# The last 256 features of a feed-forward input product, as a narrow seven-product group

## The chip, the cores and the metric

One Trainium2 chip, one of its cores. The metric is the device time of one execution in microseconds (us). The kernel before took 850.61 us (median of 3 runs, 849.67 to 852.32).

## The reference, cut to what matters

One decoder layer on 512 tokens of width 1024: a mixer block of three branches, merged and put through `w_out`, and then a feed-forward part (FFN) with 2816 hidden features.

```python
x = x + merged @ w_out[l]                      # (512, 1024)
h2 = rmsnorm(x, norm_ffn_g[l])
ffn_g, ffn_u = jnp.split(h2 @ w_ffn_in[l], 2, axis=-1)      # 1024 -> 2 x 2816
x = x + (jax.nn.silu(ffn_g) * ffn_u) @ w_ffn_out[l]         # 2816 -> 1024
return rmsnorm(x, final_norm_g)
```

All of it is float32. A product of two float32 matrices is computed in three terms of a shorter type (float32r): each operand is split into a rounded part `hi` and a remainder `lo`, and hi x hi, hi x lo and lo x hi are added up.

## The kernel before, in words

The kernel is a list of operations with their dependences. A planner in the kernel file (`schedule`, L253) gives every operation an engine, a start by its own table of costs, and a buffer, and the program then runs each engine's list in that fixed order. Priorities set by `at(...)` decide between operations that could start at the same time.

Weights come in units of 512 KB (128 partitions x 1024 numbers). A unit is loaded by a DMA on SP's queue into a buffer called `raw` (two of them) or `ch` (six), cast to `hi` by ScalarE (ACT in the profile) and subtracted to `lo` by VectorE (DVE) (`unit_loads`, L529). There are three buffers for `hi` and three for `lo`, so the cast of a unit waits until TensorE (PE) is done with the unit three before it.

The FFN's input product runs as a seven-product scheme (Strassen's, in Winograd's form): the tokens are cut in two halves of 256, the 1024 inputs in two halves, and a group of 512 gate features and the 512 up features that belong to them are the two halves of the output. Seven products of halves take the place of eight (`PRODUCTS`, L98, in the order p1, p3, p5, p2, p6, p7, p4). Their input operands are the normalized tokens (`xh`, `xl`) and sums of them (`c1`, `c2`), made on VectorE and split once. Their weight operands are sums of blocks of `w_ffn_in`. These sums are made by the DMA: a plain load of one block into a `ch` buffer, and later accumulating DMAs on POOL's queue (GpSimd) that add further blocks (`accum`, L456). In an ordinary group two such running sums serve all products: x for p1, p5, p6, p4 and y for p3, p7; p2 is a plain load (`_group`, L68). Each is two units wide, so a group has 14 units, and a unit 12 matmuls of 128 x 512: two token tiles, two blocks of 128 inputs, three terms (`seven`, L1159). An accumulation into a running sum has to wait until the split of the sum's last state is done.

Products are collected in PSUM: p1 with p6 and p3 with p7 in tiles called `g`, p5 with p4 and p2 in tiles called `m`. `evict` (L1206) reads them out, applies the row norms `rstd2`, Silu and the gate product, and 16 transposes per group bring the result to features on partitions (`feat`, tiles `a`), with copies by ScalarE.

Five groups make 2560 features. The last 256 features (`LEFT`, features 20 and 21 of 128) run before the groups as plain products over all 512 tokens (L1133): gate and up for each, four products of 24 matmuls of 128 x 512, with the row norms broadcast to `RB2` (L1125 to L1128) and the result written straight to `feat`.

The output product follows in two sections of the same scheme (`SECTIONS`, L90), the first over features 0 to 11 of 128, the second over 12 to 21. Its operands are made from the tiles `a` in buffers `R` (36 of them). 32 of the 36 hold the input product's operands, so most become free only as the last group of the input product is done with them.

Of the kernel before, what the change touches and what calls it, by code (L numbers as in the profile page):

```python
# [13 lines left out]
ALU = mybir.AluOpType  # L14
AX = mybir.AxisListType

P = 128
# [3 lines left out]
KD = 8  # L21
DFF = 2816
# [14 lines left out]
UNITS = []  # L37


def _units():  # L40
# [12 lines left out]
    for d in W_OUT:  # L53
        UNITS.append(("col", "w_out", d * P))
    for f in LEFT:
        UNITS.append(("col", "w_ffn_in", f * P))
        UNITS.append(("col", "w_ffn_in", DFF + f * P))
    for n in range(len(UNITS)):
        STREAM.append(("raw", n, 2))

    for g in range(5):
        _group(g, "w_ffn_in", [[(4 * h + 2 * j, 4 * h + 2 * j + 1) for j in range(2)] for h in range(2)],
               (g * 512, DFF + g * 512))
    for s, halves in enumerate(SECTIONS):
        _group(5 + s, "w_ffn_out", halves, (0, 512))
# [18 lines left out]

LEFT = (20, 21)
W_OUT = (0, 4, 1, 5, 2, 6, 3, 7)
# [11 lines left out]
STREAM = []  # L100
# [374 lines left out]
def tile_block(ctx: ExitStack, tc: tile.TileContext, xT_d, w_d, wif_d, pp_d, nb_d, fg_d, cf_d, cm_d, out_d):  # L475
# [53 lines left out]
    def unit_loads():  # L529
        chains, before = {}, []  # L530
        for u, (kind, w, width, *more) in enumerate(STREAM):
            parts = []
            for n, sl in enumerate([slice(0, 512), slice(512, 1024)] if u < 2 else [slice(0, 512 * width)]):
# [3 lines left out]
                with at(URGENT, -1, u + 0.2 * n):  # L537
                    if kind == "add":
                        raw = chains[more[0]]
                        E.accum(raw, w_d[w, :, sl])  # L540
                    else:
                        raw = new("F" if u < 2 else "ch" if kind == "new" else "raw", f"raw{u}_{n}", shape)
                        E.load(raw, w_d[w, :, sl])
# [548 lines left out]
    rstd2 = const("rstd2", [P, NC])  # L1092
    acc2, RB2 = tmp("sqacc2"), keep("RB2")
    for n, d in enumerate(W_OUT):
# [29 lines left out]
    with at(URGENT, 0):  # L1124
        rms_cols(acc2, rstd2, "ffn")  # L1125
        rb2 = psm("rb2")
        bcast_cols(rb2, rstd2)
        E.copy(RB2, rb2)  # L1128


    av = [new("a", f"a{i}", (P, 2, S)) for i in range(KF // 2)]
    feat = [av[f // 2][:, f % 2, :] for f in range(KF)]
    for f in LEFT:  # L1133
        g, u = tmp(f"ffsg{f}"), tmp(f"ffsu{f}")
        for nm, t in (("g", g), ("u", u)):
            p = psg(f"ff{nm}{f}")
            hi, lo = unit()
            product(p, hi, lo, xh, xl, KD, alloc=[t])
            with at(URGENT, 0):
                E.tt(t, p, RB2, ALU.mult)  # L1140
        with at(CHAIN):
            E.act(g, g, "Silu")
            E.tt(feat[f], g, u, ALU.mult)

    x2n = [[xr[i * 4 + c] for i in range(2)] for c in range(NC)]
# [12 lines left out]

    def seven(tag, widths, operand, evict, by_token=False):  # L1159

# [3 lines left out]
        for name, op, m in PRODUCTS:  # L1164
            for j, w in enumerate(widths):
                hi, lo = unit()
                ah, al = operand(op, j)
                if by_token and name == PRODUCTS[-1][0]:
                    last.append((j, w, hi, lo, ah, al))
                    continue  # L1170
                with at(GEMM, count[1]):
                    for t in range(2):
                        for kk in range(w):
                            sl = slice(kk * 512, (kk + 1) * 512)
                            first = j == kk == 0
                            fresh = name in ("p1", "p3", "p5", "p2")
                            E.mm(acc[m][t], ah(kk, t), hi[:, sl], first and fresh, False, skip=not fresh)
                            E.mm(acc[m][t], ah(kk, t), lo[:, sl], False, False, skip=not fresh)
                            E.mm(acc[m][t], al(kk, t), hi[:, sl], False,
                                 j == len(widths) - 1 and kk == w - 1, skip=not fresh)  # L1180
            for t in range(2):
                for j, w, hi, lo, ah, al in last:
                    with at(GEMM, count[1]):
                        for kk in range(w):
                            sl = slice(kk * 512, (kk + 1) * 512)
                            for a, b in ((ah, hi), (ah, lo), (al, hi)):
                                end = b is hi and a is al and j == len(widths) - 1 and kk == w - 1
                                E.mm(acc[m][t], a(kk, t), b[:, sl], False, end, skip=True)
                with at(URGENT, 0):
                    evict(name, t, acc[m][t])  # L1190

    for g in range(5):
        def operand(op, j):
# [12 lines left out]
        def evict(name, t, p):  # L1206
            r1, r2 = rstd2[:, t:t + 1], rstd2[:, 2 + t:3 + t]
            if name == "p1":
                held["c11", t] = new("Y", f"c11_{g}_{t}")
                E.copy(held["c11", t], p)  # L1210
            elif name == "p3":
                held["c12", t] = tmp(f"c12_{g}_{t}")
                E.copy(held["c12", t], p)
# [6 lines left out]
            elif name == "p7":  # L1220
                x, u = held["c12", t], tmp(f"c22_{g}_{t}")
                held["c22", t] = u
# [3 lines left out]
            else:  # L1226
                x, u = tmp(f"c21_{g}_{t}"), held["c22", t]
                E.tt(x, p, u, ALU.subtract)
# [3 lines left out]

        seven(f"fi{g}", (2, 2), operand, evict)
        nat = [held[n, t] for n in ("c12", "c22") for t in range(2)]
        with at(CHAIN):
            for q in range(4):
                pt = psm(f"at{g}_{q}")
# [143 lines left out]
def _layout(inp):  # L1381
# [4 lines left out]
    for i, (kind, name, *a) in enumerate(UNITS):  # L1386
# [3 lines left out]
        elif kind == "rows":  # L1390
            pack[i] = 0
            for n, r in enumerate(a[0]):
                pack[i, :, n * 512:(n + 1) * 512] = m[r * P:(r + 1) * P, a[1]:a[1] + 512]
        elif kind == "nat":
# [69 lines left out]
```

## Time and profile before

| | before |
|---|---|
| runs | 849.67, 850.61, 852.32 us |
| the profiled execution's own time | 851.7 us |
| its span, first to last instruction | 849.9 us |
| TensorE busy | 837.8 us (99%) |
| weight loads busy (PEld) | 694.7 us (82%) |
| VectorE busy | 644.4 us (76%) |
| ScalarE busy | 446.6 us (53%) |
| POOL busy | 60.0 us (7%) |
| mean granted clock of TensorE | 0.998 of full speed |
| DMA | 110.72 MB, 130 GB/s on average |

Matmuls are pipelined, and the duration of one includes its way through the array: 128 x 512 has a mean of 393 ns, while they follow each other much faster. So what counts for the time is the distance from one start to the next, which is read from the timeline or the chain of waits by dividing a stretch by its count. In the chain the name before a line number is the tile that is written: "PE g L374" are matmuls of `mm` into tiles `g`, "PE m L380" are transposes. Names of tiles are without their numbers: R are operands in float32r, hi and lo the halves of the weights.

### The profile page before, as it was taken

To read this page: it belongs to the slowest core of one execution; us is meant where nothing else is said; L and a number is where in the kernel's file an instruction comes from. 1 tells how busy PE (TensorE), PEld (TensorE's weight loads), DVE (VectorE), ACT (ScalarE), POOL (GpSimd) and SP (SyncE) were. 2 spreads that over 40 slices of the span, in tenths; PEclk is the share of its full clock that TensorE was granted. 3 is DMA by queue.
4 is the path that set the end of the run, shared out by engine and by line. 5 is a ranking of instruction groups with operands and counts; after the bars stand their busy time and mean duration, and the time that the engine had idled before them with its cause. 6 is when DMAs were issued, how large, how long until landed. Compare 5 with 4: busy or idle time off the path is not lost.

```text
span 849.9 us, 10774 instructions
## 1 busy us (share of the span) xinstructions
PE 837.8 (99%) x3952; PEld 694.7 (82%) x3952; DVE 644.4 (76%) x1139; ACT 446.6 (53%) x702; POOL 60.0 (7%) x76
## 2 busy tenths in 40 slices
PE   8999999999999999999999999999999999999996
PEld 6888888888878888888888888888888888888875
DVE  7868899999999985226228686476757578989977
ACT  6355243334798984331333565446454657655545
POOL 1000000000000000000000000212121212121220
PEclk9999999999999999999999999999999999999999
DMA  9322122222221223322225722779798988797773
GB/s 320 128 73 84 51 75 75 75 76 81 92 98 52 76 74 99 100 93 83 101 96 198 246 100 73 137 190 179 187 180 189 179 184 181 196 207 187 149 131 117
DMA packets 33748, 110.72 MB, mean 130 GB/s; under 512 B 3744, under 2 KB 4128, under 8 KB 33696
## 3 DMA queue, kind: packets, MB, share of 16 engines
q1 hardware_dynamic: 24480, 77.53, 27.1%
q0 software_dynamic: 9216, 32.51, 22.0%
q8 instruction: 31, 0.51, 0.3%
q14 instruction: 21, 0.17, 0.1%
HBM read 107.93 MB, written 2.10 MB: 129 GB/s over the span
## 4 chain that ended last, share of the span: by engine, by line
PE 94%; DVE 4%; DMA 1%; issue 0%; ACT 0%; SPq 0%; ACTq 0%; DVEq 0%
PE g L374 71%; PE m L374 20%; PE m L380 2%; DVE xf L412 1%; DVE lo L405 1%; DMA raw<-in_w_dram 1%; DVE R L405 1%; DMA F<-in_w_dram 1%; DVE F L412 0%; ACT hi L396 0%; DVE R L430 0%; DVE xf L420 0%; SPq L453 0%; DVE T L405 0%; DVE F L405 0%
## 5 line engine op out<-in xcount | busy, mean ns | idle before, releaser
L374 PE MATMUL g<-R,hi 128*128 128x512 f32 x1200 | 298.7, 393 | 0.0
L374 PEld LDWEIGHTS g<-R,hi 128*128 128x128 f32 x1200 | 222.5, 188 | 44.3
L405 DVE TENSOR_TENSOR lo<-raw,hi 128x1024 fp32r<-128x1024 f32 x98 | 119.2, 1216 | 97.1 <-PE g L374 63.2
L374 PE MATMUL g<-hi,R 128*128 128x512 f32 x608 | 187.3, 393 | 0.9 <-DVE lbt L434 0.9
L396 ACT CAST hi<-raw 128x1024 fp32r<-128x1024 f32 x98 | 102.6, 1047 | 160.0 <-PE g L374 120.3
L374 PE MATMUL g<-R,lo 128*128 128x512 f32 x600 | 157.9, 395 | 0.0
L405 DVE TENSOR_TENSOR lo<-ch,hi 128x1024 fp32r<-128x1024 f32 (+1 forms) x96 | 113.7, 1188 | 53.7 <-ACT hi L396 46.4
L396 ACT CAST hi<-ch 128x1024 fp32r<-128x1024 f32 (+1 forms) x96 | 98.2, 1024 | 89.6 <-PE g L374 39.0
L374 PEld LDWEIGHTS g<-hi,R 128*128 128x128 f32 x608 | 114.3, 189 | 24.4 <-ACT T L389 1.1
L374 PEld LDWEIGHTS g<-R,lo 128*128 128x128 f32 x600 | 111.1, 188 | 21.8
L374 PE MATMUL m<-hi,R 128*128 128x512 f32 x372 | 118.4, 391 | 0.1
L374 PE MATMUL g<-lo,R 128*128 128x512 f32 x304 | 114.7, 397 | 0.0
L459 POOL DMA_DIRECT2D ch<-in_w_dram x64 | 55.6, 878 | 687.4 <-DVE lo L405 687.4
L374 PEld LDWEIGHTS m<-hi,R 128*128 128x128 f32 x372 | 69.9, 188 | 14.7 <-ACT hi L396 0.5
L374 PE MATMUL m<-lo,R 128*128 128x512 f32 x186 | 73.0, 392 | 0.2 <-DVE lo L405 0.2
L374 PEld LDWEIGHTS g<-lo,R 128*128 128x128 f32 x304 | 57.7, 190 | 11.9 <-DVE lo L405 0.3
L412 DVE SCALAR_TENSOR_TENSOR xf<-xf,pp,xf 128x511 f32<-128x511 f32 (+29 forms) x60 | 42.6, 725 | 0.1
L396 ACT CAST R<-T 128x512 fp32r<-128x512 f32 (+1 forms) x48 | 28.3, 601 | 27.4 <-DVE T L405 11.5
L374 PEld LDWEIGHTS m<-lo,R 128*128 128x128 f32 x186 | 34.9, 188 | 7.4 <-DVE lo L405 0.5
L389 ACT ACT_TABLE_LOAD x31 | 39.8, 1283 | 1.2 <-PEq L1453 0.7
L405 DVE TENSOR_TENSOR R<-T,R 128x512 fp32r<-128x512 f32 (+1 forms) x48 | 30.8, 662 | 0.7 <-ACT R L396 0.7
L389 ACT ACTIVATE xf<-g,pp 128x512 f32<-128x512 f32 x27 | 18.6, 690 | 15.6 <-PE g L374 15.5
(207 smaller groups left out, 800.6 us busy)
## 6 DMA issues: line engine op xcount, KB each, us to landing
raw<-in_w_dram SPq DMA_DIRECT2D x97, 512.0 KB, 3.3
ch<-in_w_dram POOLq DMA_DIRECT2D x60, 512.0 KB, 5.5
ch<-in_w_dram SPq DMA_DIRECT2D x30, 512.0 KB, 4.5
F<-in_xT_dram SPq DMA_DIRECT2D x12, 256.0 KB, 4.9
out_dram<-F SPq DMA_DIRECT2D x8, 256.0 KB, 2.1
F<-in_w_dram SPq DMA_DIRECT2D x4, 256.0 KB, 5.5
xf<-in_xT_dram SPq DMA_DIRECT2D x4, 256.0 KB, 7.0
xf<-in_cm_dram SPq DMA_DIRECT2D x4, 256.0 KB, 5.2
```

What stands on the lines that cost most here:

```text
L374: return self.pr.add("PE", cost, [lhsT, rhs, *after], [out], lambda: self.nc.tensor.matmul(r(out), lhsT=r(lhsT), rhs=r(rhs), start=start, ...
L380: lambda: self.nc.tensor.transpose(r(out), r(in_), r(ident)))
L389: lambda: self.nc.scalar.activation(r(out), r(in_), getattr(AF, func), bias=r(bias), scale=r(scale), **{k: r(x) for k, x in kw.items()}),
L396: lambda: self.nc.scalar.copy(out=r(out), in_=r(in_)))
L405: return self.pr.add("V", (66 + free_size(out)) / 0.96, [a, b, *after], [out], lambda: self.nc.vector.tensor_tensor(out=r(out), in0=r(a), ...
L412: lambda: self.nc.vector.scalar_tensor_tensor(r(out), r(a), r(s), r(b), op0=op0, op1=op1))
L459: return self.pr.add("G", 1000.0, [out], [out], lambda: self.nc.gpsimd.dma_start(out=r(out), in_=src, accum_op=ALU.add), lat=_prod(out.sha ...
```

## The change

The features 20 and 21 are no longer computed by plain products ahead of the groups. They become a sixth group at the end of the input product, of 256 gate and 256 up features, with the same seven products. Its unit holds four blocks of 128 inputs x 256 features, so a product has one unit and 24 matmuls of 128 x 256. Each product's weight sum is made by itself: a load of the first block and accumulating DMAs for the others, one for p5 and p7, two for p6, three for p4, none for p1, p3 and p2. The broadcast of the row norms goes, and the evictions and 8 transposes of the new group come, with half-width tiles. The planner makes a new order of everything from the end of the `w_out` product on.

```diff
-    for f in LEFT:
-        UNITS.append(("col", "w_ffn_in", f * P))
-        UNITS.append(("col", "w_ffn_in", DFF + f * P))
...
+    _last_group((5 * 512, DFF + 5 * 512))
...
+def _last_group(cols):
+    b = [[], []]
+    for h in range(2):
+        for n in range(2):
+            b[h].append(len(UNITS))
+            UNITS.append(("rows", "w_ffn_in", range(4 * h, 4 * h + 4), cols[n], 256))
+    (b11, b12), (b21, b22) = b
+    blocks = dict(p1=[b11], p3=[b22], p5=[b11, b12], p2=[b21], p6=[b11, b12, b22], p7=[b12, b22],
+                  p4=[b11, b12, b22, b21])
+    for prod, _, _ in PRODUCTS:
+        STREAM.append(("sum", blocks[prod], 2))
...
+                    elif kind == "sum":
+                        raw = new("ch" if len(w) > 1 else "raw", f"raw{u}_{n}", shape)
+                        E.load(raw, w_d[w[0], :, sl])
+                        for more in w[1:]:
+                            E.accum(raw, w_d[more, :, sl])
...
-        rb2 = psm("rb2")
-        bcast_cols(rb2, rstd2)
-        E.copy(RB2, rb2)
...
-    for f in LEFT:
-        g, u = tmp(f"ffsg{f}"), tmp(f"ffsu{f}")
-        for nm, t in (("g", g), ("u", u)):
-            p = psg(f"ff{nm}{f}")
-            hi, lo = unit()
-            product(p, hi, lo, xh, xl, KD, alloc=[t])
-            with at(URGENT, 0):
-                E.tt(t, p, RB2, ALU.mult)
-        with at(CHAIN):
-            E.act(g, g, "Silu")
-            E.tt(feat[f], g, u, ALU.mult)
...
-    def seven(tag, widths, operand, evict, by_token=False):
+    def seven(tag, widths, operand, evict, by_token=False, cols=512):
...
+                w = w * 512 // cols
...
-                            E.mm(acc[m][t], ah(kk, t), hi[:, sl], first and fresh, False, skip=not fresh)
+                            E.mm(acc[m][t][:, :cols], ah(kk, t), hi[:, sl], first and fresh, False, skip=not fresh)
...
-    for g in range(5):
+    for g in range(6):
+        cols = 512 if g < 5 else 256
...
-        seven(f"fi{g}", (2, 2), operand, evict)
+        seven(f"fi{g}", (2, 2) if g < 5 else (2,), operand, evict, cols=cols)
...
-            for q in range(4):
+            for q in range(cols // P):
```

How the order moves, at three places. On TensorE, the end of the `w_out` product (its last matmul is the row that reads lo_1_81) and what follows; before, first the left-over feature 20, whose weights hi stand behind the tokens R:

```order
L374 MATMUL g_2_85<-R_25_132,lo_1_81 128x512
L374 MATMUL g_3_86<-R_30_137,hi_2_79 128x512
L380 MATMUL m_1_88<-cf_59,F_7_150 128x128
L380 MATMUL m_1_88<-cf_59,F_3_146 128x128
L380 MATMUL m_1_88<-cf_59,F_9_152 128x128
L380 MATMUL m_3_90<-cf_59,F_7_150 128x128
L380 MATMUL m_3_90<-cf_59,F_3_146 128x128
L380 MATMUL m_3_90<-cf_59,F_9_152 128x128
L374 MATMUL g_3_86<-R_32_139,hi_2_79 128x512
```

The same place now:

```order
L385 MATMUL g_2_85<-R_25_132,lo_1_81 128x512
L385 MATMUL g_3_86<-hi_2_79,R_30_137 128x512
L391 MATMUL m_1_88<-cf_59,F_7_150 128x128
L391 MATMUL m_1_88<-cf_59,F_3_146 128x128
L391 MATMUL m_1_88<-cf_59,F_9_152 128x128
L391 MATMUL m_3_90<-cf_59,F_7_150 128x128
L391 MATMUL m_3_90<-cf_59,F_3_146 128x128
L391 MATMUL m_3_90<-cf_59,F_9_152 128x128
L385 MATMUL g_3_86<-lo_2_82,R_30_137 128x512
```

The matmuls between the transposes of the residual are now those of p1 of the first group (hi and lo are the moving operand, the token tile R the weights of the array).

On POOL's queue, the accumulating DMAs of group 4 (the fifth) and what lies around them; before, p5 (ch_0, ch_1), p7 (ch_2, ch_3), p6 and p4 (ch_0, ch_1 twice), and then the output product's first (ch_4):

```order
L459 DMA ch_0_3492<-in_w_dram 128x1024
L459 DMA ch_1_3493<-in_w_dram 128x1024
L459 DMA ch_2_3494<-in_w_dram 128x1024
L459 DMA ch_3_3495<-in_w_dram 128x1024
L459 DMA ch_0_3492<-in_w_dram 128x1024
L459 DMA ch_1_3493<-in_w_dram 128x1024
L459 DMA ch_0_3492<-in_w_dram 128x1024
L459 DMA ch_1_3493<-in_w_dram 128x1024
L459 DMA ch_4_3496<-in_w_dram 128x1024
```

The same place now, up to the last one of the new group:

```order
L470 DMA ch_4_3496<-in_w_dram 128x1024
L470 DMA ch_0_3492<-in_w_dram 128x1024
L470 DMA ch_5_3497<-in_w_dram 128x1024
L470 DMA ch_1_3493<-in_w_dram 128x1024
L470 DMA ch_2_3494<-in_w_dram 128x1024
L470 DMA ch_5_3497<-in_w_dram 128x1024
L470 DMA ch_3_3495<-in_w_dram 128x1024
L470 DMA ch_0_3492<-in_w_dram 128x1024
L470 DMA ch_1_3493<-in_w_dram 128x1024
L470 DMA ch_0_3492<-in_w_dram 128x1024
L470 DMA ch_1_3493<-in_w_dram 128x1024
L470 DMA ch_2_3494<-in_w_dram 128x1024
L470 DMA ch_3_3495<-in_w_dram 128x1024 x3
```

The new group's sums for p5 (ch_4, once) and p6 (ch_5, twice) lie between those of group 4; its p7 (ch_2) and the three of p4 (ch_3) come behind them.

On TensorE, the end of the new group's p4 and the start of the output product, now:

```order
L385 MATMUL m_1_88<-lo_0_80,R_1_108 128x256
L385 MATMUL m_1_88<-hi_0_77,R_5_112 128x256
L385 MATMUL m_1_88<-hi_0_77,R_24_131 128x256
L391 MATMUL m_2_89<-cf_59,T_4_157 128x128
L391 MATMUL m_0_87<-cf_59,T_4_157 128x128
L385 MATMUL m_1_88<-lo_0_80,R_24_131 128x256
L385 MATMUL m_1_88<-hi_0_77,R_27_134 128x256
L385 MATMUL g_3_86<-hi_1_78,R_16_123 128x512
L385 MATMUL g_3_86<-lo_1_81,R_16_123 128x512
```

The output product's p1 follows the last matmul of the new p4 directly, where before it followed group 4's p4.

## Rows read from the trace of the kernel before

**Rows 1.** From the page: busy time of each engine, and the shares of the chain that ended last, by engine.

```profile
PE 837.8 (99%) x3952; PEld 694.7 (82%) x3952; DVE 644.4 (76%) x1139; ACT 446.6 (53%) x702; POOL 60.0 (7%) x76
PE 94%; DVE 4%; DMA 1%; issue 0%; ACT 0%; SPq 0%; ACTq 0%; DVEq 0%
```

**Rows 2.** From the chain of waits in order of time (start, duration, what, how many): p5 and p2 of one group, its p6 and p7, and p5 and p2 of the next.

```profile
627.31 10.88 PE m L374 x48
638.19 10.88 PE g L374 x48
...
667.34 10.88 PE m L374 x48
```

**Rows 3.** The windows of the second to the fifth group of the input product and of the output product's first section: stretch and length, busy time and count of PE, PEld, DVE, ACT and POOL, granted clock, share of the DMA engines, GB/s.

```profile
576.30:616.30 40.00, 40.00 (x186) 33.01 (x185) 27.07 (x31) 22.17 (x29) 6.92 (x8) 1.00 0.86 184
616.30:656.30 40.00, 40.00 (x186) 33.00 (x185) 25.76 (x29) 21.23 (x27) 6.91 (x8) 1.00 0.85 184
656.30:696.40 40.10, 40.10 (x186) 33.09 (x185) 25.85 (x29) 21.33 (x28) 6.93 (x8) 1.00 0.87 185
696.40:736.40 40.00, 40.00 (x186) 32.94 (x185) 37.13 (x49) 26.49 (x37) 6.91 (x8) 1.00 0.84 190
736.40:793.60 57.20, 57.20 (x259) 47.40 (x258) 53.41 (x73) 34.77 (x50) 9.51 (x11) 1.00 0.80 181
```

**Rows 4.** The timeline of PE over the left-over features (start, duration of the merged row, line, operation, tiles, shape, count); the first row is their first matmul, the last the first one of the groups.

```profile
511.54 0.39 PE L374 MATMUL g<-R,hi 128*128 128x512 f32 x1
511.77 0.82 PE L380 MATMUL m<-cf,F 128*128 128x128 f32 x6
...
512.66 0.49 PE L380 MATMUL m<-cf,F 128*128 128x128 f32 x3
...
514.84 0.60 PE L380 MATMUL m<-cf,F 128*128 128x128 f32 x4
...
516.90 0.95 PE L374 MATMUL m<-cf,T 128*128 128x1 f32 x8
517.71 1.88 PE L374 MATMUL g<-R,lo 128*128 128x512 f32 x7
...
525.10 0.60 PE L380 MATMUL m<-cf,rstd 128*128 128x128 f32 x4
525.46 3.69 PE L374 MATMUL g<-R,hi 128*128 128x512 f32 x15
...
536.24 0.39 PE L374 MATMUL g<-hi,R 128*128 128x512 f32 x1
```

**Rows 5.** The timeline of PE in the mixer, where narrow matmuls stand in a row between wide ones.

```profile
274.96 1.28 PE L374 MATMUL m<-sp,T 128*128 128x130 f32 x10
275.99 0.71 PE L374 MATMUL g<-R,hi 128*128 128x512 f32 x2
276.54 0.40 PE L374 MATMUL m<-R,R 128*128 128x256 f32 x2
276.78 0.40 PE L374 MATMUL g<-R,hi 128*128 128x512 f32 x1
```

**Rows 6.** From the groups of instructions by shape: all matmuls of 256 columns, and the weight loads of the commonest group (count, busy us, mean ns of one, idle before).

```profile
L374 PE MATMUL m<-R,R 128*128 128x256 f32 x8 | 1.7, 292 | 0.0
...
L374 PEld LDWEIGHTS g<-R,hi 128*128 128x128 f32 x1200 | 222.5, 188 | 44.3
```

**Rows 7.** The DMA answer for the five groups, 536.24 to 736.4: packets, MB and share of 16 engines' time of POOL's queue (q0) and SP's (q1), and the issues with KB each and the median us to landing.

```profile
q0 software_dynamic: 5655, 20.61, 59.8%
q1 hardware_dynamic: 4464, 15.99, 23.8%
...
ch<-in_w_dram POOLq DMA_DIRECT2D x40, 512.0 KB, 5.3
ch<-in_w_dram SPq DMA_DIRECT2D x20, 512.0 KB, 4.4
raw<-in_w_dram SPq DMA_DIRECT2D x10, 512.0 KB, 4.5
```

**Rows 8.** The timeline of the queues of POOL and SP around group 4 (696.4 to 736.4): its first accumulating DMA, and the four loads into ch behind its p7 and p4 units.

```profile
692.02 0.86 POOL L459 DMA_DIRECT2D ch<-in_w_dram  x1 [12.86 <-DVE lo L405]
...
720.67 8.54 SPq L453 DMA_DIRECT2D ch<-in_w_dram  x4
```

**Rows 9.** From the groups of instructions by shape on DVE and ACT (count, busy us, mean ns of one): the subtraction and the cast of a weight unit in ch, and the split of an operand of the output product.

```profile
L405 DVE TENSOR_TENSOR lo<-ch,hi 128x1024 fp32r<-128x1024 f32 x90 | 110.0, 1222 | 53.7 <-ACT hi L396 46.4 <-PE g L374 6.9
L405 DVE TENSOR_TENSOR R<-T,R 128x512 fp32r<-128x512 f32 x44 | 29.3, 684 | 0.3 <-ACT R L396 0.3
...
L396 ACT CAST hi<-ch 128x1024 fp32r<-128x1024 f32 x90 | 94.5, 1051 | 89.0 <-PE g L374 38.7 <-PE m L374 33.5 <-issue 12.6
```

**Rows 10.** From the answer on the tiles ch, 500 to 820.

```profile
DMA to landing us min/median/max: 2.6/5.3/8.7
```

**Rows 11.** The timeline of DVE at the end of the `w_out` product: its last residual pass, a pass of 256 columns, and the last split of a token sum.

```profile
512.94 0.68 DVE L405 TENSOR_TENSOR F<-g,F 128x512 f32<-128x512 f32 x1
...
516.94 0.42 DVE L405 TENSOR_TENSOR T<-T 128x256 f32<-128x256 f32 x1
...
520.84 0.68 DVE L405 TENSOR_TENSOR R<-T,R 128x512 fp32r<-128x512 f32 x1
```

More of the change, by code (lines that the diff above doesn't have):

```diff
@@ L83, in _group @@
                            "p2": ("raw", b21, w)}[prod])
-LEFT = (20, 21)
+def _last_group(cols):
[9 more added lines that the diff above has]
+        STREAM.append(("sum", blocks[prod], 2))
 W_OUT = (0, 4, 1, 5, 2, 6, 3, 7)
@@ L1092, in tile_block @@
     rstd2 = const("rstd2", [P, NC])
-    acc2, RB2 = tmp("sqacc2"), keep("RB2")
+    acc2 = tmp("sqacc2")
     for n, d in enumerate(W_OUT):
@@ L1173, in seven @@
                         for kk in range(w):
-                            sl = slice(kk * 512, (kk + 1) * 512)
+                            sl = slice(kk * cols, (kk + 1) * cols)
                             first = j == kk == 0
                             fresh = name in ("p1", "p3", "p5", "p2")
-                            E.mm(acc[m][t], ah(kk, t), hi[:, sl], first and fresh, False, skip=not fresh)
-                            E.mm(acc[m][t], ah(kk, t), lo[:, sl], False, False, skip=not fresh)
-                            E.mm(acc[m][t], al(kk, t), hi[:, sl], False,
+                            E.mm(acc[m][t][:, :cols], ah(kk, t), hi[:, sl], first and fresh, False, skip=not fresh)
+                            E.mm(acc[m][t][:, :cols], ah(kk, t), lo[:, sl], False, False, skip=not fresh)
+                            E.mm(acc[m][t][:, :cols], al(kk, t), hi[:, sl], False,
                                  j == len(widths) - 1 and kk == w - 1, skip=not fresh)
@@ L1187, in seven @@
                                 end = b is hi and a is al and j == len(widths) - 1 and kk == w - 1
-                                E.mm(acc[m][t], a(kk, t), b[:, sl], False, end, skip=True)
+                                E.mm(acc[m][t][:, :cols], a(kk, t), b[:, sl], False, end, skip=True)
                 with at(URGENT, 0):
-                    evict(name, t, acc[m][t])
-    for g in range(5):
+                    evict(name, t, acc[m][t][:, :cols])
+    for g in range(6):
+        cols = 512 if g < 5 else 256
         def operand(op, j):
@@ L1208, in evict @@
             if name == "p1":
-                held["c11", t] = new("Y", f"c11_{g}_{t}")
+                held["c11", t] = new("Y", f"c11_{g}_{t}", (P, cols))
                 E.copy(held["c11", t], p)
             elif name == "p3":
-                held["c12", t] = tmp(f"c12_{g}_{t}")
+                held["c12", t] = tmp(f"c12_{g}_{t}", (P, cols))
                 E.copy(held["c12", t], p)
@@ L1220, in evict @@
             elif name == "p7":
-                x, u = held["c12", t], tmp(f"c22_{g}_{t}")
+                x, u = held["c12", t], tmp(f"c22_{g}_{t}", (P, cols))
                 held["c22", t] = u
@@ L1226, in evict @@
             else:
-                x, u = tmp(f"c21_{g}_{t}"), held["c22", t]
+                x, u = tmp(f"c21_{g}_{t}", (P, cols)), held["c22", t]
                 E.tt(x, p, u, ALU.subtract)
@@ L1391, in _layout @@
             pack[i] = 0
+            c = a[2] if len(a) > 2 else 512
             for n, r in enumerate(a[0]):
-                pack[i, :, n * 512:(n + 1) * 512] = m[r * P:(r + 1) * P, a[1]:a[1] + 512]
+                pack[i, :, n * c:(n + 1) * c] = m[r * P:(r + 1) * P, a[1]:a[1] + c]
         elif kind == "nat":
```

## The prediction

> **What bounds the kernel now.** I read the page first, then the chain of waits, then the timeline of single stretches, then the DMA answer. The page gives TensorE 837.8 us busy in a span of 849.9, and the chain that ended last lies 94% on it [rows 1]. The reader should see in the chain of waits that the FFN part is one unbroken string of matmuls: a group of the input product, from its p5 to the next group's p5, takes 667.34 - 627.31 = 40.03 us, and 48 matmuls of 512 columns take 10.88, so 0.2267 us each [rows 2]. A group has 168 of them (38.08 us) and 16 transposes, which get what is left: 1.95 us, 0.122 each. So the time follows from the count and the pitch of the matmuls, as long as nothing arrives late. Beside TensorE the DMA engines are busy at 0.84 to 0.87 of these windows, and VectorE rises to 37.1 of 40.0 us when the operands of the output product are made [rows 3]. These two can turn a saving on TensorE into a wait.
>
> **What goes.** The two left-over features are four products of 24 matmuls, 96 of 512 columns. In the timeline they are the rows from 511.54 to 536.24, with other work between them [rows 4]; 96 x 0.2267 = 21.76 us. The broadcast of the row norms (four transposes, 525.10 to 525.46) goes too, 0.36 us. The 13 transposes of the residual and the 8 column sums that lie in the same stretch stay and move into the first group. Four weight units (loads, casts, subtractions), six VectorE multiplies, three ScalarE passes go as well; all lay beside matmuls and give nothing back.
>
> **What comes.** Seven products, two token halves, four blocks, three terms: 168 matmuls of 256 columns, 24 to a weight unit. The same form (128x256, both operands of the same type, a weight load before each) stands in the trace eight times [rows 5, 6]. From 276.54 to 276.78, when the next matmul starts, two of them took 0.238 us: 0.119 each. Bounds: never under the 0.103 at which ten matmuls of 130 columns follow each other (274.96 to 275.99), each with a load of its own; never over the 0.188 that a weight load lasts [rows 6], if loads could not overlap. I take 0.119, the form's own pitch: 168 x 0.119 = 19.99 us. With the bounds it is 17.3 and 31.6. Eight transposes come at 0.122 each, 0.97 us.
>
> On TensorE alone: -21.76 - 0.36 + 19.99 + 0.97 = **-1.16 us**. One seven-product group saves an eighth of the multiplications, but it pays a fixed part per matmul twice as often: 0.2267 / 2 is 0.113, and 0.119 is what 256 columns cost.
>
> [...]
>
> **The weights of the new group.** A sum of blocks is now made afresh for each product: 7 loads and 7 accumulating transfers of 512 KB, against 4 plain loads that go. Over the five groups the accumulating queue took 59.8% of 200.2 us for 20.61 MB, or 39.3 units: 3.04 us of all 16 engines for a unit; the plain queue 23.8% for 15.99 MB, 30.5 units: 1.56 us [rows 7]. The new group costs 7 x 3.04 + 7 x 1.56 = 32.2 us of DMA time beside 168 x 0.119 + 0.97 = 21.0 us of TensorE. An ordinary group needs 8 x 3.04 + 6 x 1.56 = 33.7 us beside 40.0. So the new one is over its own time by 11 us, and must live on what starts early. It can: the buffers of p5 and p6 are those that group 3 gives back, so these sums start before group 4 begins, and p1 and p3 are plain loads into buffers free since group 4's p2.
>
> On POOL's queue the new transfers are put between those of group 4, and an instruction that waits there holds what stands behind it. The first (for p5) waits for its load, and behind it stands group 4's own p5, at 692.02 before [rows 8]; that transfer is needed only where group 4's p5 begins, 696.4 + 10.9 = 707.3, less a cast of 1.05 and a subtraction of 1.22 [rows 9], so it has some 7 us beyond its landing time of 5.3.
>
> The longest new chain is p4's: one load, then three accumulating transfers, each waiting for the one before. Its buffer comes free with group 4's second p7 unit, in the row of four loads from 720.67 [rows 8], the second about 2.7 later: 723.4. With the median landing times 4.4 and 5.3 [rows 7] it is done at 723.4 + 4.4 + 3 x 5.3 = 743.7, cast and split by 746.1. TensorE wants it at 736.4 + 6 x 24 x 0.119 + 8 x 0.122 = 754.5 on this axis. With the longest landing of a unit in these buffers, 8.7 [rows 10], for all four it would be 758.2 and split at 760.5, 6 us late. I take the medians: nothing.
>
> **VectorE and ScalarE.** The new group has 7 splits of 1.22 us [rows 9] and 14 passes of 256 columns at 0.42, the time of such a pass [rows 11]: 14.4 us of VectorE in 21.0. The operands of the output product could start in group 4's p1 before, because that was the last use of its input tiles; now that is the new group's p1, so what VectorE does for p1, p3 and p5 (nine sums and nine splits of 0.68, 12 us [rows 9]) has six units of 2.86 and six of 2.72, 33 us, until p5 instead of 18 units of 2.72, 49 us. From 696.4 to 793.6 VectorE had 90.5 us of work in 97.2 [rows 3]; with the new group 104.9 in 118.2. The average falls, and I cost it at nothing; without that slack a late split stops TensorE for its 1.22.
>
> **The start of the first group.** The left-over products were cover: while they ran, VectorE and ScalarE made the last operand sums. The last residual pass ran at 512.94, the last split for p3 from 520.84 to 521.52 [rows 11]. Without the cover TensorE reaches the second half of p3 after 36 matmuls, 13 transposes and the column sums (516.90 to 517.71 [rows 4]): 511.54 + 8.2 + 1.6 + 0.8 = 522.1, half a microsecond after that split ended. I allow 0.2 us; without any margin it would be up to 2.
>
> Sum: -1.16 + 0.2 = -1.0 us. The profiled execution took 851.7 (span 849.9), 1.1 over the median of the runs, 850.61. I put the difference on the median: **849.6 us**.
>
> **Rivals.**
> - *Shorter pitch.* In a long run of 256-column matmuls the pitch falls towards that of the narrow ones, 0.108 say. For: each measured pair has a 512-column neighbour. Against: 0.119 also holds from the pair's second into its neighbour. Price: 168 x 0.011 = 1.8 more, so -2.8: 847.8, 0.33% faster. Chance 0.15.
> - *DMA engines full* (the slower side). Group 4 and the new group together need 33.7 + 32.2 = 65.9 us of DMA in 61.0 us of TensorE. If the queues cannot begin early enough, the missing 4.9 us become waits in front of the new group's p7 and p4: -1.0 + 4.9 = +3.9, 854.5. It decides when p4's chain lands later than 752. For: the share is 0.84 to 0.87 already. Against: two of the sums start in group 3's shadow, and 0.80 in the window after leaves room [rows 3]. Chance 0.17, a little less of it beyond 0.3%.
> - *The weight load is the bound.* The loads add up to 694.7 us, 82% of the span [rows 1]. If a matmul cannot follow its predecessor faster than a load lasts, 168 x 0.188 = 31.6 and the change is 10.6 us slower: 861.2. The 103 ns of rows 5 speak against it, beside loads of 188 that overlap. Chance 0.03. The Trainium skill, Perfetto Trace Analysis, section Identifying the Most-Contended Engine, calls the busy share of weight loads a good measure of TensorE's headroom; by that rule this rival is the one to expect. The trace does not agree, for the same 103 ns.
> - *The lost cover costs 2 us* at the start of the first group: 851.4, no measurable change. Chance 0.10.
>
> **How the numbers follow.** Forecast 0.55, rivals 0.15, 0.17, 0.03 and 0.10. A measurement of this kernel can tell 0.3%, 2.55 us: 848.06 to 853.16. Faster: the shorter pitch and a twentieth where the forecast's own terms and the noise of the runs (849.67 to 852.32) add up, 0.20. Slower: most of the DMA rival, the load rival and a small part of the forecast, 0.20. The rest, 0.60, is no change. The forecast's own range is 848.0 to 851.5; the range that holds 8 in 10 reaches from the shorter pitch less 0.8 of noise, 847.0, to the DMA rival, 854.5.
>
> **What the profile after would show.** The sum is right if between the last 512-column matmul of group 4 and the first of the output product there are about 21 us, 2.86 to a unit of 24; a unit of 2.6 is the shorter pitch, 4.5 the load rival. The DMA rival shows as idle of TensorE there, released by VectorE's subtraction for p7 or p4 after a late DMA, and by landing times over 7 us on POOL's queue. The lost cover shows as idle before p3 of the first group, ended by VectorE or ScalarE. I am wrong on the main point if the stretch is near 21 us with TensorE unbroken and the whole is still more than 2.5 us off: then the time went to a place that I cost at nothing.

## The result and the profile after

| | before | after |
|---|---|---|
| runs | 848.88 to 852.32 us, median 850.14 (4) | 856.27 to 858.55 us, median 857.16 (4) |
| ratio | | 1.0081, 95% interval 1.0067 to 1.0095 |
| profiled execution, its span | 851.7, 849.9 us | 856.98, 854.8 us |

The change makes the kernel 7.0 us slower. The forecast was 849.6, with a range from 847.0 to 854.5.

From the page of the kernel after, the rows that answer to [rows 1]:

```profile
PE 837.8 (98%) x4028; PEld 696.7 (82%) x4028; DVE 648.4 (76%) x1150; ACT 450.6 (53%) x712; POOL 66.1 (8%) x83
PE 81%; DVE 8%; DMA 5%; issue 3%; ACT 1%; POOL 0%; SPq 0%; ACTq 0%; POOLq 0%; DVEq 0%
```

TensorE is busy as long as before, and yet the chain that ended last now lies only 81% on it. Something else is waited for. To see where, cut the program at two places that both kernels have: p5 of the first group of the input product (48 matmuls with p2) and p5 of the output product's first section (72 matmuls with p2). The chain of waits, in order of time, has both. Before:

```profile
57.33 5.44 PE m L374 x24
...
547.28 10.88 PE m L374 x48
...
752.83 16.32 PE m L374 x72
```

After:

```profile
55.95 5.44 PE m L385 x24
...
523.68 10.88 PE m L385 x48
...
670.85 10.61 DMA ch<-in_w_dram
...
684.17 11.85 DMA ch<-in_w_dram
...
702.00 5.35 DMA ch<-in_w_dram
...
708.75 9.02 issue
...
718.66 5.33 issue
...
724.01 7.53 DMA ch<-in_w_dram
...
731.63 1.05 ACT hi L407
...
732.71 0.95 DVE lo L416
...
756.15 16.32 PE m L385 x72
```

The three parts of the span:

| part | before | after | difference |
|---|---|---|---|
| start to the first group's p5 | 547.28 | 523.68 | -23.60 |
| from there to the output product's p5 | 205.55 | 232.47 | +26.92 |
| from there to the end of the span | 97.07 | 98.65 | +1.58 |

In the first part 1.38 us are not the change's: the same 24 matmuls of the mixer begin at 57.33 before and at 55.95 after. In the profiles of all the runs below this start lies between 55.49 and 57.36, so it is taken out. The left-over products gave back 22.22 us. The sixth group was to cost 20.96 and took 26.92. The end is 1.58 later.

The middle part holds the loss. The windows of the kernel after, in the columns of [rows 3]:

```profile
667.00:697.00 30.00, 30.00 (x141) 24.56 (x140) 15.99 (x17) 14.46 (x19) 8.49 (x10) 1.00 0.98 205
697.00:732.00 35.00, 33.64 (x223) 30.32 (x221) 26.37 (x34) 17.78 (x27) 4.35 (x5) 1.00 0.96 253
732.00:734.00 2.00, 0.40 (x2) 0.20 (x2) 1.29 (x2) 2.00 (x4) 0.00 (x0) 1.00 0.04 8
734.00:736.00 2.00, 2.00 (x14) 2.00 (x15) 2.00 (x4) 1.50 (x2) 0.00 (x0) 0.83 0.53 150
736.00:738.00 2.00, 1.80 (x9) 1.50 (x8) 2.00 (x6) 0.00 (x0) 0.86 (x1) 0.50 0.28 113
738.00:740.00 2.00, 1.95 (x9) 1.76 (x10) 2.00 (x4) 0.44 (x2) 0.58 (x1) 0.82 0.84 113
```

The DMA engines are full, at 0.98 and 0.96, for the 65 us from 667 to 732. At 732 to 734, where TensorE mostly stands, they have almost nothing to do (0.04): the last weights of the sixth group have landed by then. What TensorE waited for in the FFN: us in all, times, the longest:

```profile
PE m L385 <- ACT hi L407: 1.3, 1, 1.3
PE m L385 <- DVE lo L416: 1.1, 2, 0.9
PE g L385 <- DVE lo L416: 0.9, 2, 0.8
PE m L391 <- DVE T L423: 0.3, 1, 0.3
```

The first two rows are the sixth group's p4, at 731.24. The third is p6 of group 4, at 697.31; it waits for an addition that was issued at 684.17 and landed 11.85 later. In the answer on the tiles ch, 664 to 735, the row that answers to [rows 10] reads:

```profile
DMA to landing us min/median/max: 3.2/7.1/11.8
```

The chain of p4 is the one whose end was worked out in the prediction. Its load, issued at 702.00, took 5.35. Then POOL's queue shows the three additions; the bracket is POOL's idle time and what ended it:

```profile
707.88 0.86 POOL L470 DMA_DIRECT2D ch<-in_w_dram  x1 [0.66 <-DMA ch<-in_w_dram]
717.78 0.88 POOL L470 DMA_DIRECT2D ch<-in_w_dram  x1 [9.04 <-DMA ch<-in_w_dram]
724.01 0.88 POOL L470 DMA_DIRECT2D ch<-in_w_dram  x1 [5.34 <-DMA ch<-in_w_dram]
```

Each waits for the one before. The chain of waits shows the first two only as "issue" behind POOL (708.75 and 718.66), and the third as the DMA of 7.53. It ends at 731.53. TensorE's timeline around it:

```profile
725.48 0.28 PE L385 MATMUL g<-hi,R 128*128 128x256 f32 x1
...
731.12 0.28 PE L385 MATMUL g<-hi,R 128*128 128x256 f32 x1
732.73 0.38 PE L385 MATMUL m<-hi,R 128*128 128x256 f32 x1 [1.33 <-ACT hi L407]
733.99 0.38 PE L385 MATMUL m<-lo,R 128*128 128x256 f32 x1 [0.88 <-DVE lo L416]
734.21 0.40 PE L385 MATMUL m<-hi,R 128*128 128x256 f32 x2
734.45 0.28 PE L385 MATMUL m<-lo,R 128*128 128x256 f32 x1
...
735.89 0.63 PE L385 MATMUL m<-hi,R 128*128 128x256 f32 x2
736.32 0.41 PE L385 MATMUL m<-lo,R 128*128 128x256 f32 x1
736.53 0.63 PE L385 MATMUL m<-hi,R 128*128 128x256 f32 x2
```

Two things are to be read here. From 725.48 to 731.12 there are 47 distances, 0.120 each: that is the pitch of the narrow matmul. And from 735.3 on, three of them take 0.64 instead of 0.36 (735.89 to 736.53): the clock granted is 0.50 from 736 to 738, which is the 1.2 GHz level. Before that, TensorE had stood still for most of the 2.9 us from 731.12 to 733.99. From 734.21 the other 22 matmuls of p4 and two transposes take 4.65 us up to the first of the output product at 738.86; at full pitch they would take 2.86, and 0.25 is a short wait for VectorE. So a wait of 2.2 us in p4 brought about 1.5 us of slow matmuls with it. The Trainium skill, TensorE: Matmul & The Clock Gate, Part 1, says that a gate lets through half of the pulses, 1.2 of 2.4 GHz, when the array has not been busy; the trace agrees with the two levels.

The end. In VectorE's timeline the last operand of the output product before, and then after:

```profile
810.07 0.41 DVE L405 TENSOR_TENSOR R<-a,R 128x256 fp32r<-128x256 f32 x1
```

```profile
839.00 0.42 DVE L416 TENSOR_TENSOR R<-a,R 128x256 fp32r<-128x256 f32 x1
```

TensorE ends at 842.2 before and at 846.0 after. So this operand stood 32 us ahead of TensorE's end, and now 7: VectorE makes operands among the last evictions, and the stretch behind TensorE's last matmul grew from 7.7 to 8.8 us. The chain of waits says the same. Before, it lies on TensorE up to the last matmul:

```profile
835.41 6.81 PE m L374 x30
842.25 0.69 DVE F L405
```

After, it lies on VectorE from 823.57 to the end; one row of it:

```profile
840.07 1.82 DVE lo L416 x2
```

### The profile page after: what moved, and what is told of

Same layout as the page of the kernel before. It is cut to its first block, busy times and chain, and to the rows that moved or that the text cites. A ratio compares the mean times of both kernels' runs of the same rounds, so it can differ in the third digit from the quotient of the medians.

```text
span 854.8 us, 10972 instructions
## 1 busy us (share of the span) xinstructions
PE 837.8 (98%) x4028; PEld 696.7 (82%) x4028; DVE 648.4 (76%) x1150; ACT 450.6 (53%) x712; POOL 66.1 (8%) x83
## 4 chain that ended last, share of the span: by engine, by line
PE 81%; DVE 8%; DMA 5%; issue 3%; ACT 1%; POOL 0%; SPq 0%; ACTq 0%; POOLq 0%; DVEq 0%
PE g L385 61%; PE m L385 18%; DMA ch<-in_w_dram 5%; DVE lo L416 2%; PE m L391 2%; DVE xf L423 1%; DVE F L416 1%; DVE R L416 1%; DVE T L416 1%; ACT hi L407 1%; DMA F<-in_w_dram 1%; DVE F L423 1%; DVE R L423 1%; POOL ch L470 0%; SPq L464 0%
## 5 line engine op out<-in xcount | busy, mean ns | idle before, releaser
L385 PE MATMUL g<-R,hi 128*128 128x512 f32 x1136 | 282.4, 393 | 0.0
L385 PEld LDWEIGHTS g<-R,hi 128*128 128x128 f32 x1136 | 210.7, 188 | 42.0
L385 PE MATMUL g<-hi,R 128*128 128x512 f32 (+1 forms) x672 | 199.2, 382 | 0.9 <-ACT T L400 0.9
L416 DVE TENSOR_TENSOR lo<-raw,hi 128x1024 fp32r<-128x1024 f32 (+1 forms) x97 | 118.0, 1216 | 94.4 <-PE g L385 63.1
L407 ACT CAST hi<-raw 128x1024 fp32r<-128x1024 f32 (+1 forms) x97 | 101.5, 1047 | 164.8 <-PE g L385 120.2
L385 PEld LDWEIGHTS g<-hi,R 128*128 128x128 f32 x672 | 123.7, 188 | 24.1 <-ACT R L412 1.0
L385 PE MATMUL m<-hi,R 128*128 128x512 f32 (+1 forms) x420 | 128.5, 382 | 1.3 <-ACT hi L407 1.3
L385 PE MATMUL g<-lo,R 128*128 128x512 f32 (+1 forms) x336 | 123.6, 385 | 0.9 <-DVE lo L416 0.9
L385 PEld LDWEIGHTS m<-hi,R 128*128 128x128 f32 x420 | 78.3, 191 | 16.2 <-ACT hi L407 1.8
L385 PE MATMUL m<-lo,R 128*128 128x512 f32 (+1 forms) x210 | 80.5, 383 | 1.1 <-DVE lo L416 1.1
```

Source lines behind the costliest of these rows:

```text
L385: return self.pr.add("PE", cost, [lhsT, rhs, *after], [out], lambda: self.nc.tensor.matmul(r(out), lhsT=r(lhsT), rhs=r(rhs), start=start, ...
L407: lambda: self.nc.scalar.copy(out=r(out), in_=r(in_)))
L416: return self.pr.add("V", (66 + free_size(out)) / 0.96, [a, b, *after], [out], lambda: self.nc.vector.tensor_tensor(out=r(out), in0=r(a), ...
```

## The experiments

Three theories were set against each other. A: the DMA engines are full, and any product may be the one that is late. B: only the serial chain of p4's four transfers is too long. C: the place of the group, last before the output product, makes VectorE late. All runs below stand beside runs of the kernel before on the same chip (medians 850.64 to 850.95).

**The additions left out.** `E.accum` of the sixth group keeps its place in the plan and issues nothing:

```diff
-        return self.pr.add("G", 1000.0, [out], [out], lambda: self.nc.gpsimd.dma_start(
+        return self.pr.add("G", 1000.0, [out], [out], lambda: skip or self.nc.gpsimd.dma_start(
...
-                            E.accum(raw, w_d[more, :, sl])
+                            E.accum(raw, w_d[more, :, sl], True)
```

> The kernel after with the seven accumulating transfers of the sixth group left out (its loads stay, the planned order stays; so the sums of weight blocks in p5, p6, p7 and p4 of that group are incomplete and its features wrong). Theory A, the 16 DMA engines are full from 667 to 731: 7 x 3.04 = 21.3 us of DMA time go, TensorE's waits in front of group 4's p7 (1.2) and of the sixth group's p4 (2.6), the half clock behind them (about 1) and part of the late end (1 to 1.5) go: 850.5 to 852. Theory B, only the serial chain of four transfers for p4 is too long: the wait before group 4's p7 stays, 852 to 853.5. Theory C, it is the place of the group at the end of the input product that makes VectorE late, whatever the DMA does: 855 to 857.

Measured: 851.03 us, ratio 0.9998 (0.9989 to 1.0007). Theory A's range; B's and C's are missed. The expectation says p7 of group 4 where it is p6. In the chain of waits:

```profile
524.71 10.88 PE m L385 x48
...
719.53 5.76 PE m L385 x48
725.29 5.76 PE g L385 x48
731.05 2.64 PE m L385 x22
...
751.25 16.32 PE m L385 x72
```

No row but TensorE's, 0.120 for each narrow matmul, and from p5 to p5 226.54: 20.99 more than before. The sum of the prediction for TensorE alone was 20.96. So the waits and the slow clock behind them are 232.47 - 226.54 = 5.93 us of the kernel after. What is left of the loss is the end: it is still 1.1 us later than before, of the 1.58, so most of that is not the additions'.

**The same transfers, shorter chain for p4.**

```diff
-    blocks = dict(p1=[b11], p3=[b22], p5=[b11, b12], p2=[b21], p6=[b11, b12, b22], p7=[b12, b22],
-                  p4=[b11, b12, b22, b21])
+    blocks = dict(p1=[b11], p3=[b22], p5=[b11, b12, b22], p2=[b21], p6=[b11, b12, b22, b21], p7=[b12, b22],
+                  p4=[b11, b12])
```

> The kernel after with the same number of transfers for the sixth group, but two of p4's three accumulations given to p5 and p6 (5: two, 6: three, 7: one, 4: one; the sums are then wrong, and with them that group's features). Theory A (engines full): the same bytes have to land before the same time, so some product of the sixth group is late as before, 2 to 4 us of waits in all: 855.5 to 858.5. Theory B (p4's serial chain): p4 is one load and one accumulation, its wait of 2.6 and the half clock behind it go: 852 to 853.5. Theory C: 857.

Measured: 855.71 us, 1.0061 (1.0049 to 1.0073). Theory A; B falls. The waits in the FFN:

```profile
PE g L385 <- ACT hi L407: 2.6, 1, 2.6
PE g L385 <- DVE lo L416: 0.5, 1, 0.5
```

p4 no longer waits. Now group 4's own p6 waits longer, because more of the sixth group's additions were issued ahead of its own and held one of them for 15.07 us, from issue to landing:

```profile
680.66 15.07 DMA ch<-in_w_dram
```

From p5 to p5 it is 231.87 by the starts in the timeline, against 232.47: with the same bytes the loss is nearly the same and has only changed its place. Again slow matmuls follow the wait: the granted clock is 0.55 from 699 to 701 and 0.60 from 701 to 703.

**Plain transfers in place of the additions.**

```diff
-            out=r(out), in_=src, accum_op=ALU.add), lat=_prod(out.shape) * 4 / 210.0)
+            out=r(out), in_=src, **({} if plain else dict(accum_op=ALU.add))), lat=_prod(out.shape) * 4 / 210.0)
...
-                            E.accum(raw, w_d[more, :, sl])
+                            E.accum(raw, w_d[more, :, sl], True)
```

> The kernel after with the sixth group's seven accumulating transfers turned into plain ones of the same size on the same queue in the same place (they overwrite, so the sums are wrong). If the bytes and the number of transfers fill the DMA engines: no change, 856 to 858. If it is the addition that makes a transfer twice as dear (3.04 against 1.56): 7 x 1.5 = 10.4 us of DMA go, the waits too, 851 to 853.

Measured: 850.81 us, 1.0003 (0.9993 to 1.0012). So neither the bytes nor the number of transfers fill the engines, but the addition does. POOL's queue from 667 to 732 (packets, MB, share of 16 engines), after, and then in this run:

```profile
q0 software_dynamic: 2160, 7.87, 66.9%
```

```profile
q0 software_dynamic: 2192, 8.00, 54.3%
```

After, 7.87 MB are 15.0 units of 0.524 MB, all added: 0.669 x 65 / 15.0 = 2.90 us of 16 engines each. In this run 8.00 MB are 15.3 units, 7 of them plain: (0.543 x 65 - 8.3 x 2.90) / 7 = 1.6 us each, what a plain load cost in [rows 7]. These prices add up the times of the packets, which can overlap: from 674 to 689 of the kernel after, POOL's queue alone moves data, 3.10 MB or 5.9 units, and its share reads 106.3%; so there an addition passes every 2.5 us. The Trainium skill, DMA: Bandwidth & Descriptors, Rules for kernel authors, says that an accumulating DMA reads its destination and writes it later; nearly twice the engine time for the same bytes fits that, though no run here shows the read itself.

**Running sums.** The three runs above leave the weight sums of the sixth group incomplete or form others; this one computes everything. p6 adds one block to p5's sum, and p4 one to p6's.

```diff
-        STREAM.append(("sum", blocks[prod], 2))
+        x, y = ("x", 5, 0), ("y", 5, 0)
+        STREAM.append({"p5": ("sum", blocks["p5"], 2, x), "p6": ("add", b22, 2, x), "p4": ("add", b21, 2, x)}.get(
+            prod, ("sum", blocks[prod], 2, y)))
...
+                        chains[more[0]] = raw
```

> The kernel after with one running sum for p5, p6 and p4 of the sixth group, as the ordinary groups have it (p6 adds one block to p5's sum, p4 one to p6's): 2 loads and 3 accumulations fewer, all results as before. Theory A (DMA full): 2 x 1.56 + 3 x 3.04 = 12.2 us of DMA go, more than the 11 by which the sixth group was over its own time, so the waits shrink to under 1 us in all and the time comes near that of the run without the accumulations: 851 to 853. Against it: p4's addition now has to wait for the split of p6, and if that latency (5.3 for the transfer, 2.3 for cast and split) does not fit in the 5.7 us between p6 and p4, a wait of 1 to 3 us stands before p4: 853 to 855.

Measured: 850.95 us, 1.0007 (0.9997 to 1.0017), no wait over 0.2 us in the input product. With 12 us of DMA less the waits are gone, as A has it.

**The place.** The left-over products, plain, at the end of the input product; the sixth group ahead of the last ordinary one; and without the sixth group.

```diff
-    for f in LEFT:
-        g, u = tmp(f"ffsg{f}"), tmp(f"ffsu{f}")
...
                 E.copy(feat[4 * g + q], pt)
+
+    for f in LEFT:
+        g, u = tmp(f"ffsg{f}"), tmp(f"ffsu{f}")
```

> The kernel before with the four plain products of features 20 and 21 moved from the start of the input product to its end (same matmuls of 512 columns, same loads, nothing else). Theory A and B: 4 plain loads, 6 us of DMA beside 22 us of TensorE, nothing waits: 849.5 to 851.5. Theory C (the place): the operands of the output product are late and the end is 1.5 to 3 us later: 852 to 853.5. If the left-over products were needed as cover at the start, that also shows here, as idle of TensorE before p3 of the first group.

Measured: 849.31 us, 0.9992 (0.9983 to 1.0001), just under the range of A and B and far from C's; TensorE is without a wait from 480 on. Cover was not needed, and work at this place is not late by itself.

```diff
+GROUPS = (0, 1, 2, 3, 5, 4)
...
-    for g in range(6):
+    for g in GROUPS:
```

> The kernel after with the sixth group ahead of the last ordinary group instead of behind it, nothing else. Theory A (DMA full): its surplus of 11 us of DMA stands between two groups that leave 6 us each, so waits of 2 to 5 us remain, now in groups 3 to 5; what came late on VectorE at the end (1.8) goes, as group 4 is again the last: 853 to 856. If only the place at the end mattered: 849 to 850.

Measured: 856.53 us, 1.0072 (1.0052 to 1.0091), half a microsecond above what A gave. Waits for weights are back, 2.5 us in all, in p6 of group 3 and in p4 of the sixth group; others, 1.9 us, are for tiles T of VectorE and a copy by ScalarE. From the first group's p5 to the output product's it is 232.47 again, as in the kernel after. The last operand of the output product is made at 813.17, 32 us ahead of TensorE's end, as before: the late end does go with the last place, and the waits for DMA don't.

```diff
-    _last_group((5 * 512, DFF + 5 * 512))
...
+    av[10] = av[9]
...
-    for g in range(6):
+    for g in range(5):
```

> The kernel after without the sixth group (features 20 and 21 are left out; the output product reads 18 and 19 in their place). All theories: what goes is worth 22.1 us plus nothing for lost cover: 827.5 to 828.5. Then the sixth group costs 29 us against the 21 of its matmuls and transposes. If the left-over products were cover for the start, 829 or more.

Measured: 827.51 us, 0.9733 (0.9720 to 0.9745). The time is at the lower end of what was expected. The removal is worth 23.2 us against 850.7, 1.1 more than the 22.1; the sixth group then costs 857.16 - 827.51 = 29.7 us for 21 us of TensorE.

**More buffers R**, on the run with running sums:

```diff
-N_R, N_F, N_A, N_Y, N_CH, N_XF, N_SP, N_T, LEAVE = 36, 10, 11, 2, 6, 21, 4, 10, 4
+N_R, N_F, N_A, N_Y, N_CH, N_XF, N_SP, N_T, LEAVE = 38, 9, 11, 2, 6, 22, 4, 9, 4
```

> The run with running sums, with 38 buffers R instead of 36 (one T and one F fewer make room, one more of the early F). In that run the DMA waits are gone, and what is left against the forecast is 1.8 us at the end, where VectorE still makes operands of the output product. Theory C1, these are late because the last group of the input product holds 32 of the 36 buffers R: with 38 the operands move up (six instructions in VectorE's order) and a part of the 1.8 goes: 849.0 to 850.3. Theory C2, VectorE simply has 14 us more work there: no change, 850.5 to 851.5.

Measured: 849.92 us, 0.9988 (0.9979 to 0.9997). The last operand moves up, from 824.5 in the run with running sums to:

```profile
814.10 0.42 DVE L418 TENSOR_TENSOR R<-a,R 128x256 fp32r<-128x256 f32 x1
```

and the stretch behind TensorE's last matmul is 7.7 us again (9.0 in the run without); the chain of waits lies on TensorE up to its last matmul again. That is theory C1 against C2: VectorE's work is the same, and other numbers of buffers are enough to have it done in time, so it was not too much. That it is R is argued, not shown, as T, F and the early F (N_XF) changed with it. Nor does the time of the last operand alone set the end: with running sums it stood 15.8 us ahead of TensorE's end, against 7.0 in the kernel after, and the stretch behind was 9.0 against 8.8.

**The sixth group first.** Its weights fall where the DMA engines have room: from 480 to 520 they are at 0.29 in the kernel before and at 0.40 in the kernel after. Of the kernel after only the order of the groups changes, and in the first, third and fourth of these runs the order of the new group's products, to p1, p2, p3, p5, p6, p7, p4. The third and fourth add the running sums and the 38 buffers.

```diff
+GROUPS = (5, 0, 1, 2, 3, 4)
...
+LAST = tuple(PRODUCTS[i] for i in (0, 3, 1, 2, 4, 5, 6))
...
-    for g in range(6):
+    for g in GROUPS:
```

> The kernel after with the sixth group as the first of the six, in the order p1, p2, p3, p5, p6, p7, p4, so that p1 and p2 need only the tokens themselves. The DMA engines are at 0.29 to 0.40 there. Theories A, B and C all expect the waits to go: the group costs 20 to 21 us where the left-over products cost 22.1, so 849.0 (848 to 850). The rival that the left-over products were cover: the sums of the operands come too late for p3 or p5, 850.5 to 853. If the narrow matmuls themselves cost more than 0.119 each, the time is over 850 with TensorE unbroken.

Measured: 849.00 us, 0.9981 (0.9971 to 0.9991): faster than the kernel before, by 0.8 to 2.5 us, with the 1.16 of the prediction's sum for TensorE inside. The engines are nearly full here too, at 0.96 from 470 to 500, but ahead of need: the last addition lands at 504.05, and p4 begins at 529.56. So what costs is not the full engines but a landing later than its matmuls.

> The sixth group first as before in these runs, but with its products in the usual order p1, p3, p5, so that the sums of operands are wanted 2.9 us after the start instead of 5.8. If the left-over products were needed as cover, TensorE waits 0.5 to 3 us before p3 or p5: 849.5 to 852. If the planned order fills that gap with other matmuls: 849.0, as with p2 second.

Measured: 850.38 us, 0.9999 (0.9988 to 1.0011). There is one wait, and it is not at p3 or p5:

```profile
496.55 0.66 PE L394 MATMUL m<-cf,F 128*128 128x128 f32 x4 [1.20 <-DVE F L419]
```

It is a transpose of the residual in the `w_out` product, which the planner put elsewhere. So the cover rival falls here by its place, as TensorE does not wait before p3 or p5, though the time lies in its range. Where the 1.4 us against the run before come from is open: the execution profiled here has this wait of 1.20 and took 849.35, no more than the 849.74 of the one profiled there.

> The sixth group first, in the order p1, p2, p3, and with running sums for p5, p6 and p4 (3 accumulations and 2 loads fewer). All theories: the DMA engines are not full there, so the 12 us of DMA saved are worth nothing: 849.0, the same as without running sums, or up to 1 us more if p4's addition waits for p6's split.

Measured: 852.48 us, 1.0026 (1.0014 to 1.0039), a miss: 3.5 us slower than without running sums. POOL's queue:

```profile
518.64 0.86 POOL L476 DMA_DIRECT2D ch<-in_w_dram  x1 [42.51 <-DVE lo L422]
526.71 0.86 POOL L476 DMA_DIRECT2D ch<-in_w_dram  x1 [7.21 <-DVE lo L422]
```

An addition to a running sum starts only when the sum's last state is split. With separate sums they had landed long before; here they land as TensorE comes to them, and it waits several times in the group. Fewer bytes are worth nothing where the engines have room, and the wait is new.

> The sixth group first, in the order p1, p2, p3, with 38 buffers R. Group 4 is the last group here, as in the kernel before, where the order of VectorE's operands does not move with 38 buffers: 849.0 (848 to 850). Theory C1 allows a gain only if the single waits of 0.5 in the output product go with it: 848.

Measured: 849.35 us, 0.9981 (0.9971 to 0.9992): nothing to gain, as the operands were not late.

## Why the prediction was wrong

*What goes*: right. Worth 22.22 us by the first part of the span, where 22.12 less 0.2 stood. The lost cover cost nothing that a run showed.

*What comes*: right. 0.120 a matmul where 0.119 was taken, and 20.99 for the group with its transposes where 20.96 was. The rivals of the shorter pitch and of the weight load as the bound fall with that. The lower bound of 0.103 was itself misread: ten matmuls have nine distances among themselves, and the merged row of 1.28 less the last one's 0.275 gives 0.112 each; so the shorter pitch of 0.108 lay below even that of 130 columns.

*The weights of the new group*: wrong, and this is the step that decided. The sum stood there: 32.2 us of DMA beside 21.0 of TensorE, 11 us over; and in the rival, 65.9 us in 61.0 with group 4. The prediction then argued that what starts early makes up for it ("I take the medians: nothing"), and set p4's chain together from median landing times (4.4 and 5.3) of a stretch in which the engines were not full. On the axis of before it was to end at 743.7. It ended at 731.53 + 23.60 = 755.1, just past the 754.5 at which TensorE was to want it, with the cast and the split still to come. Three links went wrong: the load took 5.35, the additions 9.62, 5.94 and 7.53 from issue to landing, and the buffer came free at 702.00, which is 725.6 on that axis and not 723.4. Also wrong was the safety of group 4's own additions. The sum looked at its p5 alone, with 7 us to spare. It was p6 that stood behind the new group's early additions, in a queue that served them one after the other. The full-engine rival had the mechanism right, its place half right (p4, but p6 of group 4 where it said the new group's p7) and its size nearly: 4.9 us of waits where runs show 5.93, of which about 1.5 is the clock that fell behind the wait. That its size came so near is in part luck: it counts 3.04 us for an addition by its packets, and at the 2.5 us at which they pass when alone, the same sum is 15 x 2.5 + 13 x 1.56 = 57.8, below the 61.0. What the runs show is that the additions fill the engines from 667 on, and that without them, or with plain ones, TensorE does not wait in the input product. The chance of 0.17 was too low.

*VectorE*: wrong, by 1.6 us (1.1 in the run without the additions). An average of 104.9 us of work in 118.2 was to hide everything. But the last operand came 25 us later against TensorE's end, and VectorE had no slack left there. It goes with the last place, and with other numbers of buffers it is gone; that the 32 of 36 buffers R which the last group holds are the reason is likely and not shown. The range had no term for it. The three parts of the span differ from the prediction's by -0.3, +5.96 and +1.58, 7.2 us in all; the medians differ from the forecast by 857.2 - 849.6 = 7.6.

*The signs*: the waits before p4, released by VectorE (and by ACT, which was not named) behind a late DMA, and landing times over 7 us on POOL's queue were named as the mark of the full-engine rival, and they are what the profile shows.

## What to carry to other kernels

When a change asks more of a shared resource over a stretch than the stretch has, the deficit, not nothing, is the first forecast, and the way out ("it can start early") has to be shown to have room: here, by the prediction's own prices, the neighbouring group left 6 us for a surplus of 11. Landing times from an unsaturated stretch do not hold in a saturated one, and the first victim may be a neighbour whose transfers now stand behind the new ones. Before the work itself is dropped, look for another place: the same group, moved to where the engines were at 0.29 to 0.40, has the shortest time of all these kernels that compute everything (849.00 us, 0.9981). It is not clear of the noise from the left-over products at the end (849.31 us, 0.9992).

## What the runs showed of the hardware

An accumulating transfer of 512 KB takes 2.90 us of all 16 DMA engines by the sum of its packets (one passed every 2.5 us when they were alone), a plain one on the same queue about 1.6. While several additions were outstanding they landed in order (in the kernel after, seven of them between 673.98 and 688.90), so one that was issued early held up one that was wanted earlier, by up to 15.07 us. Matmuls of 256 columns, each with a weight load of its own, followed each other at 0.120 us. And a wait of TensorE of 2.2 us was followed by a stretch of 2 us at a granted clock of 0.50, in which a narrow matmul took 0.213 us instead of 0.120.
